# Late gate weights of a hybrid FoX/RWKV-7 layer: who issues the stores, when the first loads are issued, and which sums of weights a DMA makes

## The chip, the cores and the metric

The kernel runs on one core of one Trainium2 chip. The metric is the device time of one execution in microseconds; the figure that is compared is the median of several runs. For the kernel before it is 1662.03 us over 3 runs (1658.12 to 1666.03).

The engines go by the names of the profile: PE is TensorE's matmuls and PEld its weight loads, DVE is VectorE, ACT is ScalarE, POOL is GpSimd, and SP is SyncE, which here does nothing but issue DMAs. POOL and ACT can issue DMAs too. A DMA instruction stands in its engine's own in-order list: whatever it waits for, the instructions behind it on that engine wait for as well.

## The reference

One decoder layer in fp32 on 512 tokens of 2048 channels. Cut to what matters:

```python
h = rmsnorm(x, norm_gain)
u = h @ w_in                                    # 512x2048 by 2048x12488
u_fox, u_rwkv, g_a, g_b = split(u)
o_a = fox_attention(u_fox) * silu(z_a)          # 8 heads of 128, causal, forgetting
o_b = rwkv7_scan(token_shift(u_rwkv)) * silu(z_b)   # 16 heads of 64, with group norm
m = sigmoid(g_a) * (o_a @ w_proj_fox) + sigmoid(g_b) * (o_b @ w_proj_rwkv)
out = rmsnorm(x + m @ w_out, final_norm_gain)
```

The change concerns the 4096 columns of `w_in` that give g_a and g_b, the gates.

## The kernel before

Every fp32 matrix product is made of three products of fp32r tiles: each operand is split into a high part (rounded by ACT) and a low part (what is left, subtracted by DVE), and hi*hi, hi*lo and lo*hi are added up in PSUM. One product of a 128x256 block of h by a 256x512 block of weights so costs 12 matmuls of 128x128 by 128x512.

The order of the instructions of PE and SP is written by hand: generators yield after each matmul and a driver interleaves them. ACT, DVE and POOL are ordered by a scheduler that follows priorities; inside `tc.high_priority(offset=HP)` an instruction is ranked as if it stood 300 places earlier in the program. A DMA takes its place in the list of the engine that issues it by the same rule.

The program first makes the FoX and RWKV-7 branches, and then, towards 900 us, the gates, the two projections and the output product.

The gates come in four groups g of 1024 columns (g below 2 are gate B, the others gate A). A group is a 2x2 block product: two halves of the tokens, two halves of the contraction (1024 channels each) and two blocks of 512 columns. It is computed with seven products instead of eight (Strassen's scheme in Winograd's form). Two of the seven are made directly, in a stage of their own, while the last RWKV chains run: pieces of 128x512 of weights, loaded by SP, go through PE into c11, a quarter of the group. The first half of its contraction gives the partial sum p1, which is stored to DRAM (`p1_d`, L1075); after the second half tanh gives the finished quarter of the gate, stored to `sg_d` by `store_gate` (L926 to L928). Both are issued by Pool.

The other five products, the group of late units, are made by `gates_rest`. It starts once the last RWKV chain is done, since its buffers reuse that memory. A unit is 12 matmuls on a pair (hi, lo) of 128x1024 tiles, four units j=0..3 along the contraction for each of the products, which the code names by digits:

- unit 5: X = block 11 + block 12 of the weights, times the difference d1[j] of blocks of h (its tiles are named d_fqh, d_fql, d_fkh and so on, one pair for each j; d_fv stands for j=2 and d_fcb for j=3). Its PSUM tile is z.
- unit 7: block 12 + block 22, with PSUM tile x. After it block 22 is added to X.
- unit 6: that X (11 + 12 + 22), with PSUM tile y. After it Pool issues a DMA that accumulates block 21 onto X (L980).
- unit 3: block 22 once more, loaded a second time. Unit 4: X with 21 added.

In group 0 the order is (5, 7) for j=0..3, then 6 for j=0..3, then 3, then 4; the other groups go (5, 7, 6) per j. `load` (L946 to L961) brings a block of 256x512 as a tile of 128x2x512, 512 KB; the loads of the first four units (5 and 7 of j=0 and 1) are issued by Pool, the rest by SP. `prep` (L963 to L980) makes the sums and splits them (L423 casts to the high part h on ACT, L424 subtracts to the low part l on DVE). The driver prepares two units ahead and loads four ahead. The sums are `tt(V, ...)`, the helper at L482, on DVE:

```python
if p == "5":
    src = xs[j] = wp.tile([P, 2, 512], F32, tag="X", bufs=4, name=f"X_{g}{j}")
    tt(V, src, raw[n, "11"], raw[n, "12"], ALU.add)
...
if p == "7":
    tt(V, xs[j], xs[j], raw[n, "22"], ALU.add)
```

Behind units 6, 3 and 4, tanh of the sums with p1 (read back at L1002) gives the other quarters of the gate, each stored by `store_gate`. After the gates the projections `p` multiply by them: their weights are `whi_p`, `wlo_p`, and the gates are read back from `sg_d`. L136 is the matmul helper, L240 the load of a 128x512 piece (raw), L267 and L268 its split.

Of the kernel before, what the change touches and what calls it, by code (L numbers as in the profile page):

```python
# [9 lines left out]
F32 = mybir.dt.float32  # L10
F32R = mybir.dt.float32r
AF = mybir.ActivationFunctionType
ALU = mybir.AluOpType
# [4 lines left out]
P = 128  # L18
# [24 lines left out]
HP = 300  # L43
# [13 lines left out]
def hybrid_layer(  # L57
# [6 lines left out]
    nc = tc.nc  # L64
    V, S, G, PE = nc.vector, nc.scalar, nc.gpsimd, nc.tensor
# [62 lines left out]
    def mm(out, lhsT, rhs, start=True, stop=True, **kw):  # L128
        n = 1
        for d in rhs.shape[1:]:  # L130
            n *= d
        if rhs.dtype == F32R:
            clock[0] += max(n, 256) / 2370
        else:
            clock[0] += max(4 * n, {128: 514, 64: 230, 32: 150}.get(lhsT.shape[-1], 514)) / 2370
        PE.matmul(out, lhsT=lhsT, rhs=rhs, start=start, stop=stop, **kw)  # L136
# [5 lines left out]
    def ps_mm(name):  # L142
        return psm.tile([P, T], F32, tag="mm", bufs=2, name=name)
# [99 lines left out]
    def next_piece():  # L243


        i = used[0]
        used[0] += 1
        while len(raws) < min(i + (RAWS + 1 if i > 3 else 4), len(pieces)):
            raws.append(load_raw(*pieces[len(raws)]))
        split_pieces(i + (3 if i > 3 else 1))  # L250
        got = parts[i]
        parts[i] = None
        return got
# [61 lines left out]
    def gate_w(g, kb, cb, j, n=2):  # L315

        c0 = (GB0 if g < 2 else GA0) + g % 2 * 1024 + cb * 512
        r0 = (kb * KB + j * n) * P
        return w_in[r0:r0 + n * P, c0:c0 + 512]
# [24 lines left out]
    for hf in range(2):  # L344
        t = slice(256 * hf, 256 * hf + 256)
# [43 lines left out]
    for q in range(2):  # L389
        for col, base in ((0, -1), (64, 0)):  # L390
            m = smask[q * 64:(q + 1) * 64, col:col + 64]
# [29 lines left out]
    def split(hi, lo, a):  # L421

        S.copy(hi, a)  # L423
        V.tensor_tensor(lo, a, hi.bitcast(F32), ALU.subtract)  # L424
# [53 lines left out]
    sg_d = dram.tile([2, T, D], F32, name="sg_d")  # L478
    p1_d = dram.tile([4, 2, P, T], F32, name="p1_d")

    def tt(eng, o, a, b, op=ALU.mult):
        eng.tensor_tensor(o, a, b, op)  # L482
# [372 lines left out]
    def stage1():  # L855
# [69 lines left out]

        def store_gate(tile, g, th, cb, t):  # L926
            r0, c0 = 256 * th + P * t, g % 2 * 1024 + cb * 512
            G.dma_start(sg_d[g // 2][r0:r0 + P, c0:c0 + 512], tile)  # L928

        first_sums = [(w, j) for j in range(4) for w in ("d1", "s3")]  # L930
        late_stack = ExitStack()
# [11 lines left out]
        def gates_rest(wp):  # L943
# [5 lines left out]
            raw, xs, ready = {}, {}, {}  # L949
            at = [0]  # L950

            def load(upto):
                while at[0] < len(loads) and loads[at[0]][0] <= upto:
                    n, b = loads[at[0]]
                    at[0] += 1
                    g, p, j = units[n]
                    t = wp.tile([P, 2, 512], F32, tag=f"b{b}", bufs=3 if b == "22" else 2, name=f"b{b}_{g}{p}{j}")

                    (G if n < 4 else nc.sync).dma_start(
                        t, gate_w(g, int(b[0]) - 1, int(b[1]) - 1, j).rearrange("(k p) m -> p k m", p=P))  # L960
                    raw[n, b] = t  # L961

            def prep(n):  # L963
                g, p, j = units[n]
                if p == "5":
                    src = xs[j] = wp.tile([P, 2, 512], F32, tag="X", bufs=4, name=f"X_{g}{j}")
                    tt(V, src, raw[n, "11"], raw[n, "12"], ALU.add)
                elif p == "7":
                    src = raw[n - 1, "12"]
                    tt(V, src, src, raw[n, "22"], ALU.add)  # L970
                else:
                    src = raw[n, "22"] if p == "3" else xs[j]
                hi = wp.tile([P, 2, 512], F32R, tag="hi", bufs=3, name=f"h{g}{p}{j}")
                lo = wp.tile([P, 2, 512], F32R, tag="lo", bufs=3, name=f"l{g}{p}{j}")
                split(hi, lo, src)
                ready[n] = (hi, lo)
                if p == "7":
                    tt(V, xs[j], xs[j], raw[n, "22"], ALU.add)
                elif p == "6":
                    G.dma_start(xs[j], gate_w(g, 1, 0, j).rearrange("(k p) m -> p k m", p=P), accum_op=ALU.add)  # L980

            def ready_upto(n):
                while len(done) <= min(n, len(units) - 1):
# [4 lines left out]

            done = []
            load(1)  # L990
            ready_upto(1)
            yield
            left = [("s4", j) for j in range(4)]
            ev = lambda tag, nm: wp.tile([P, T], F32, tag=tag, bufs=4 if tag == "p1" else 2, name=nm)
            for n, (g, p, j) in enumerate(units):
                ready_upto(n + 2)
                load(n + 4)
                if (p, j) == ("5", 0):
                    pz = [ps_mm(f"z5_{g}_{t}") for t in range(2)]
                    p1 = [ev("p1", f"p1_{g}_{t}") for t in range(2)]  # L1000
# [12 lines left out]
                for t in range(2):  # L1013
                    for kk in range(2):
                        k = 2 * j + kk
# [38 lines left out]
        for g in range(4):  # L1054
            ps = [ps_mm(f"c11_{g}_{t}") for t in range(2)]
            for kb in range(2):
                for j in range(4):
                    ws = [next_piece(), next_piece()]
                    order = [(kk, t) for kk in range(2) for t in range(2)]
                    if j == 3:  # L1060
                        order = [(kk, t) for t in range(2) for kk in range(2)]
                    for kk, t in order:
                        k = 2 * j + kk
                        ah, al = (a[:, KB * kb + k, t * P:(t + 1) * P] for a in (hhi, hlo))
                        whi, wlo = (w[:, 0, :] for w in ws[kk])
                        for a, w, i in ((ah, whi, 0), (ah, wlo, 1), (al, whi, 2)):
                            mm(ps[t], a, w, start=kb == 0 and k == 0 and i == 0,
                               stop=kb == 1 and k == KB - 1 and i == 2, skip_group_check=True)
                            yield
                        if j == 3 and kk == 1:  # L1070
                            if kb == 0:
                                p1 = keep.tile([P, T], F32, tag=KEEP[t], name=f"p1_{g}_{t}")
                                with tc.high_priority(offset=HP):
                                    S.copy(p1, ps[t])
                                G.dma_start(p1_d[g, t], p1)  # L1075
                            else:
                                sg = keep.tile([P, T], F32, tag=KEEP[2 + t], name=f"c11_{g}_{t}")
                                with tc.high_priority(offset=HP):
                                    S.activation(sg, ps[t], AF.Tanh, scale=0.5)
                                store_gate(sg, g, 0, 0, t)  # L1080
                    if free["fox"] == 7 and first_sums:
                        sum_step(*first_sums.pop(0))
                    if g == 3 and kb == 1 and not first_sums:
                        sum_step("s2", j)
                    open_late()
# [58 lines left out]
        for br in range(2):  # L1144
            for n in range(4):
# [19 lines left out]
                for t in range(4):  # L1165
                    sg, m = sgs[br, n, t], ms_[n][:, t, :]
# [7 lines left out]

    result = []
    drive(stage1())
    mhi, mlo, turn_merged, four_banks = result

# [6 lines left out]
    for tb in range(4):  # L1185
        t = fin.tile([P, D], F32, tag="xo", bufs=4, name=f"xo_{tb}")
# [98 lines left out]
```

## Time and profile before

| | us |
|---|---|
| median of 3 runs | 1662.03 (1658.12 to 1666.03) |
| the profiled execution | 1661.46 |
| its span, first to last instruction | 1659.7 |

Shares of the span: PE 96% busy, PEld 79%, DVE 68%, ACT 47%, POOL 8%; the granted clock of TensorE is 0.99 on the mean.

The shares are means over stages with different limits, and the change touches the stretch from the last direct gate products (c, whose last matmul starts at 1054.69 us) to the end of group 0's late units and on to the projections. A row of the timeline gives the start, the length and the instruction, and in brackets the idle time of its engine before it with what ended it. PEclk is the granted clock of TensorE in shares of its full speed, the upper of its two levels (2.4 GHz; the lower is 1.2). "DMA to landing" is the time from the issue of a DMA to the arrival of its last byte. A DMA issued by Pool is in queue q0 of the page (software_dynamic), one issued by SP or ACT in a hardware queue.

### The profile page before, as it was taken

How to read it: one execution, taken by the hardware profiler on the slowest of the kernel's cores; microseconds unless marked ns; L12 is line 12 of the kernel's file. 1: busy time of each engine (PE TensorE's matmuls, PEld its weight loads, DVE VectorE, ACT ScalarE, POOL GpSimd, SP SyncE). 2: the span in 40 equal slices, each digit the busy share in tenths (PEclk: the TensorE clock that was granted, in tenths of full speed). 3: DMA queues.
4: the chain of work that ended last, by engine and by line, in shares of the span. 5: the costliest groups of instructions: out<-in, count | busy, mean ns of one | idle time of the engine just before them, and what ended most of it. 6: DMA issues, size and time to landing. Idle time of an engine off the chain costs nothing.

```text
span 1659.7 us, 23572 instructions
## 1 busy us (share of the span) xinstructions
PE 1600.1 (96%) x8378; PEld 1303.3 (79%) x8378; DVE 1127.0 (68%) x2173; ACT 771.8 (47%) x1503; POOL 132.9 (8%) x213
## 2 busy tenths in 40 slices
PE   6999899999999999999999899799999999999998
PEld 6888687787787887877878777588888787888886
DVE  6468678786787687777866859997887335544432
ACT  7533545636437446455364367554444223323322
POOL 3000000000100001000000000111111000001110
PEclk9999999999999999999999999899999999999999
DMA  5343334243333342342433366787776545463422
GB/s 168 98 104 86 82 83 106 70 112 87 93 92 85 92 113 75 95 100 68 113 84 90 102 186 186 248 251 200 235 235 172 184 153 155 151 216 122 139 83 102
DMA packets 234860, 216.39 MB, mean 130 GB/s; under 512 B 40326, under 2 KB 174062, under 8 KB 234102
## 3 DMA queue, kind: packets, MB, share of 16 engines
q1 hardware_dynamic: 222662, 179.73, 38.3%
q0 software_dynamic: 10640, 32.01, 7.0%
q10 hardware_dynamic: 1440, 3.15, 0.5%
q8 instruction: 66, 1.08, 0.3%
q14 instruction: 52, 0.43, 0.1%
HBM read 193.84 MB, written 20.99 MB: 129 GB/s over the span
## 4 chain that ended last, share of the span: by engine, by line
PE 60%; issue 15%; DVE 12%; DMA 5%; ACT 4%; POOL 2%; SPq 2%; POOLq 0%; ACTq 0%; DVEq 0%
PE o L136 11%; PE p L136 8%; PE u_fq L136 5%; PE u_fk L136 5%; PE c L136 5%; PE u_v L136 4%; PE u_z L136 4%; PE u_fv L136 3%; PE u_fz L136 3%; DVE Wt L482 3%; PE u_k L136 2%; DVE W L642 2%; PE u_r L136 1%; POOL X L980 1%; DMA lora<-in_rwkv_a_dram 1%
## 5 line engine op out<-in xcount | busy, mean ns | idle before, releaser
L136 PE MATMUL p<-whi_p,o 128*128 128x512 f32 x512 | 163.5, 396 | 0.1
L136 PEld LDWEIGHTS p<-whi_p,o 128*128 128x128 f32 x512 | 96.2, 188 | 22.2 <-ACT whi_p L267 1.0
L482 DVE TENSOR_TENSOR Wt<-W,Lt 128x16 f32<-128x16 f32 (+30 forms) x248 | 101.6, 410 | 6.2
L136 PE MATMUL p<-wlo_p,o 128*128 128x512 f32 x256 | 100.8, 394 | 1.1 <-DVE wlo_p L268 1.1
L268 DVE TENSOR_TENSOR wlo_p<-raw_p,whi_p 128x512 fp32r<-128x512 f32 x64 | 43.4, 691 | 85.6 <-ACT whi_p L267 85.5
L267 ACT ACTIVATE whi_p<-raw_p 128x512 fp32r<-128x512 f32 x64 | 40.4, 632 | 119.6 <-PE p L136 55.9
L268 DVE TENSOR_TENSOR wlo_o<-raw_o,whi_o 128x512 fp32r<-128x512 f32 x56 | 42.6, 762 | 78.0 <-ACT whi_o L267 77.5
L136 PE MATMUL o<-whi_o,mhi 128*128 128x512 f32 x224 | 87.6, 391 | 0.0
L136 PE MATMUL o<-whi_o,mlo 128*128 128x512 f32 x224 | 87.2, 389 | 0.0
L136 PE MATMUL o<-wlo_o,mhi 128*128 128x512 f32 x224 | 87.1, 389 | 0.0
L423 ACT CAST h<-X 128x1024 fp32r<-128x1024 f32 x48 | 50.5, 1052 | 65.0 <-PE z L136 22.3
L642 DVE TENSOR_REDUCE W<-Wt 128x8 f32<-128x16 f32 (+30 forms) x248 | 72.6, 293 | 5.6
L267 ACT ACTIVATE whi_o<-raw_o 128x512 fp32r<-128x512 f32 x56 | 35.3, 631 | 87.0 <-PE o L136 79.5
L424 DVE TENSOR_TENSOR l<-X,h 128x1024 fp32r<-128x1024 f32 x48 | 58.7, 1222 | 20.3 <-ACT h L423 20.1
L136 PE MATMUL c<-whi_g,hhi 128*128 128x512 f32 x128 | 53.4, 417 | 7.8 <-DVE fz L844 5.0
L719 ACT ACTIVATE pre<-SV,E 64x64 f32<-64x64 f32 x112 | 38.6, 345 | 41.8 <-DVE SV L732 40.9
L136 PEld LDWEIGHTS p<-wlo_p,o 128*128 128x128 f32 x256 | 48.1, 188 | 12.5 <-DVE wlo_p L268 2.1
L267 ACT ACTIVATE whi_g<-raw_g 128x512 fp32r<-128x512 f32 x64 | 40.2, 630 | 29.5 <-PE c L136 16.4
L423 ACT CAST h<-b 128x1024 fp32r<-128x1024 f32 x32 | 33.7, 1053 | 43.3 <-PE y L136 21.4
L268 DVE TENSOR_TENSOR wlo_g<-raw_g,whi_g 128x512 fp32r<-128x512 f32 x64 | 43.3, 685 | 14.0 <-ACT whi_g L267 13.8
L136 PE MATMUL c<-wlo_g,hhi 128*128 128x512 f32 x128 | 52.5, 410 | 0.0
L136 PE MATMUL u_fq<-hhi,whi_fq 128*128 128x512 f32 x128 | 52.4, 409 | 0.0
(428 smaller groups left out, 4711.8 us busy)
## 6 DMA issues: line engine op xcount, KB each, us to landing
b<-in_w_in_dram SPq DMA_DIRECT2D x58, 512.0 KB
raw_g<-in_w_in_dram SPq DMA_DIRECT2D x64, 256.0 KB
raw_o<-in_w_out_dram SPq DMA_DIRECT2D x56, 256.0 KB
raw_k<-in_w_in_dram SPq DMA_DIRECT2D x32, 256.0 KB
raw_r<-in_w_in_dram SPq DMA_DIRECT2D x32, 256.0 KB
raw_z<-in_w_in_dram SPq DMA_DIRECT2D x32, 256.0 KB
raw_v<-in_w_in_dram SPq DMA_DIRECT2D x32, 256.0 KB
raw_fq<-in_w_in_dram SPq DMA_DIRECT2D x32, 256.0 KB
```

The costliest lines, as they stand in the source:

```text
L136: PE.matmul(out, lhsT=lhsT, rhs=rhs, start=start, stop=stop, **kw)
L267: S.activation(whi, raw, AF.Copy)
L268: V.tensor_tensor(wlo, raw, whi.bitcast(F32), ALU.subtract)
L423: S.copy(hi, a)
L424: V.tensor_tensor(lo, a, hi.bitcast(F32), ALU.subtract)
L482: eng.tensor_tensor(o, a, b, op)
L642: V.tensor_reduce(W[:, :, i], tmp[:, :, 0:i + 1], AX.X, ALU.add)
L719: S.activation(pre[hs[q]], SV[hs[q], c, q, :], AF.Copy, scale=E1[hs[q], c, CH:CH + 1])
L980: G.dma_start(xs[j], gate_w(g, 1, 0, j).rearrange("(k p) m -> p k m", p=P), accum_op=ALU.add)
```

## The change

It has three parts.

- `store_gate` and the store of p1 are issued by ACT (`nc.scalar`) instead of Pool: 40 stores of 256 KB, 16 of them in the direct stage and 24 in the late groups.
- In group 0 block 11 is loaded straight into the tile X (four buffers, one for each j), and a second DMA, issued by Pool, accumulates block 12 onto it. Block 22 is accumulated onto X by a third one, also issued by Pool, once the split of unit 5 has read X. The DVE sums 11 + 12 and X + 22 of the four j, eight of 128x1024, are gone. Blocks 12 and 22 are still loaded plainly too, for unit 7. So there are eight accumulating DMAs more, and the number of plain loads stays.
- The loads of the first four units, with the accumulation that belongs to them, are issued at high priority.

TensorE's list is row for row the same in both kernels.

```diff
--- before.py
+++ after.py
@@ -925,7 +925,7 @@
 
         def store_gate(tile, g, th, cb, t):
             r0, c0 = 256 * th + P * t, g % 2 * 1024 + cb * 512
-            G.dma_start(sg_d[g // 2][r0:r0 + P, c0:c0 + 512], tile)
+            nc.scalar.dma_start(sg_d[g // 2][r0:r0 + P, c0:c0 + 512], tile)
 
         first_sums = [(w, j) for j in range(4) for w in ("d1", "s3")]
         late_stack = ExitStack()
@@ -954,15 +954,26 @@
                     n, b = loads[at[0]]
                     at[0] += 1
                     g, p, j = units[n]
-                    t = wp.tile([P, 2, 512], F32, tag=f"b{b}", bufs=3 if b == "22" else 2, name=f"b{b}_{g}{p}{j}")
-
-                    (G if n < 4 else nc.sync).dma_start(
-                        t, gate_w(g, int(b[0]) - 1, int(b[1]) - 1, j).rearrange("(k p) m -> p k m", p=P))
+                    onto = g == 0 and b == "11"
+                    if onto:
+                        t = xs[j] = wp.tile([P, 2, 512], F32, tag="X", bufs=4, name=f"X_{g}{j}")
+                    else:
+                        t = wp.tile([P, 2, 512], F32, tag=f"b{b}", bufs=3 if b == "22" else 2, name=f"b{b}_{g}{p}{j}")
+
+                    with tc.high_priority(offset=HP if n < 4 else 0):
+                        (G if n < 4 else nc.sync).dma_start(t, rows(g, b, j))
+                        if onto:
+                            G.dma_start(t, rows(g, "12", j), accum_op=ALU.add)
                     raw[n, b] = t
+
+            def rows(g, b, j):
+                return gate_w(g, int(b[0]) - 1, int(b[1]) - 1, j).rearrange("(k p) m -> p k m", p=P)
 
             def prep(n):
                 g, p, j = units[n]
-                if p == "5":
+                if p == "5" and g == 0:
+                    src = xs[j]
+                elif p == "5":
                     src = xs[j] = wp.tile([P, 2, 512], F32, tag="X", bufs=4, name=f"X_{g}{j}")
                     tt(V, src, raw[n, "11"], raw[n, "12"], ALU.add)
                 elif p == "7":
@@ -975,9 +986,12 @@
                 split(hi, lo, src)
                 ready[n] = (hi, lo)
                 if p == "7":
-                    tt(V, xs[j], xs[j], raw[n, "22"], ALU.add)
+                    if g == 0:
+                        G.dma_start(xs[j], rows(g, "22", j), accum_op=ALU.add)
+                    else:
+                        tt(V, xs[j], xs[j], raw[n, "22"], ALU.add)
                 elif p == "6":
-                    G.dma_start(xs[j], gate_w(g, 1, 0, j).rearrange("(k p) m -> p k m", p=P), accum_op=ALU.add)
+                    G.dma_start(xs[j], rows(g, "21", j), accum_op=ALU.add)
 
             def ready_upto(n):
                 while len(done) <= min(n, len(units) - 1):
@@ -1072,7 +1086,7 @@
                                 p1 = keep.tile([P, T], F32, tag=KEEP[t], name=f"p1_{g}_{t}")
                                 with tc.high_priority(offset=HP):
                                     S.copy(p1, ps[t])
-                                G.dma_start(p1_d[g, t], p1)
+                                    nc.scalar.dma_start(p1_d[g, t], p1)
                             else:
                                 sg = keep.tile([P, T], F32, tag=KEEP[2 + t], name=f"c11_{g}_{t}")
                                 with tc.high_priority(offset=HP):
```

Pool's list, from the store of the last RWKV output (ob_d) on, before. In the names, b11_050 is block 11 for group 0, unit 5, j=0; X_00 is the sum X of group 0, j=0; sg_d and p1_d are the gates and partial sums in DRAM.

```order
L771 DMA ob_d_559<-y_7_10521 128x512
L928 DMA sg_d_560<-c11_3_0_10726 128x512
L928 DMA sg_d_560<-c11_3_1_10735 128x512
L959 DMA b11_050_10543<-in_w_in_dram 128x2x512
L959 DMA b12_050_10545<-in_w_in_dram 128x2x512
L959 DMA b22_070_10547<-in_w_in_dram 128x2x512
L959 DMA b11_051_10745<-in_w_in_dram 128x2x512
L959 DMA b12_051_10747<-in_w_in_dram 128x2x512
L959 DMA b22_071_10755<-in_w_in_dram 128x2x512
L1002 DMA p1_0_0_10763<-p1_d_561 128x512
L1002 DMA p1_0_1_10764<-p1_d_561 128x512
L980 DMA X_00_10549<-in_w_in_dram 128x2x512
```

The same place of Pool's list in the changed kernel, where L964 is the plain load, L966 the accumulation of block 12, L990 that of block 22 and L1016 the read of p1:

```order
L771 DMA ob_d_559<-y_7_10521 128x512
L964 DMA X_00_10543<-in_w_in_dram 128x2x512
L964 DMA b22_070_10548<-in_w_in_dram 128x2x512
L964 DMA b12_050_10546<-in_w_in_dram 128x2x512
L966 DMA X_00_10543<-in_w_in_dram 128x2x512
L964 DMA X_01_10744<-in_w_in_dram 128x2x512
L964 DMA b12_051_10747<-in_w_in_dram 128x2x512
L964 DMA b22_071_10753<-in_w_in_dram 128x2x512
L966 DMA X_01_10744<-in_w_in_dram 128x2x512
L990 DMA X_00_10543<-in_w_in_dram 128x2x512
L1016 DMA p1_0_0_10762<-p1_d_561 128x512
L966 DMA X_02_10755<-in_w_in_dram 128x2x512
```

The two gate stores are gone from before the loads. The accumulations of block 12 stand between the loads, each behind the load whose tile it adds to. That of block 22 of j=0 (L990) stands ahead of that of block 12 of j=2 (L966); the next rows of the list, not shown, are the second read of p1, the accumulation of block 22 of j=1, and only then that of block 12 of j=3.

SP's list behind the last pieces of the direct stage, before:

```order
L240 DMA raw_p0_0_3_10714<-in_w_proj_rwkv_dram 128x512
L959 DMA b11_052_10757<-in_w_in_dram 128x2x512
L959 DMA b12_052_10759<-in_w_in_dram 128x2x512
L959 DMA b22_072_10785<-in_w_in_dram 128x2x512
L959 DMA b11_053_10807<-in_w_in_dram 128x2x512
L959 DMA b12_053_10809<-in_w_in_dram 128x2x512
L959 DMA b22_073_10829<-in_w_in_dram 128x2x512
L959 DMA b22_030_10922<-in_w_in_dram 128x2x512
```

And in the changed kernel:

```order
L240 DMA raw_p0_0_3_10713<-in_w_proj_rwkv_dram 128x512
L964 DMA X_02_10755<-in_w_in_dram 128x2x512
L964 DMA b12_052_10758<-in_w_in_dram 128x2x512
L964 DMA b22_072_10784<-in_w_in_dram 128x2x512
L964 DMA X_03_10804<-in_w_in_dram 128x2x512
L964 DMA b12_053_10807<-in_w_in_dram 128x2x512
L964 DMA b22_073_10827<-in_w_in_dram 128x2x512
L964 DMA b22_030_10918<-in_w_in_dram 128x2x512
```

SP's list has the same order: the load of block 11 of j=2 and 3 has become the load into X, and the first block of unit 3 (b22_030) stands behind the three loads of j=3 in both.

## Rows read from the trace of the kernel before

**Rows 1.** Stages: length, PE, PEld, DVE, ACT, POOL busy (count), PEclk, DMA share, GB/s.

```profile
1000.00:1050.00 50.00, 49.64 (x280) 39.46 (x279) 48.41 (x89) 36.86 (x69) 4.79 (x9) 1.00 0.67 198
1050.00:1100.00 50.00, 37.85 (x153) 30.22 (x152) 46.91 (x55) 22.82 (x29) 11.81 (x15) 0.86 0.76 228
1100.00:1300.00 200.00, 200.00 (x876) 164.04 (x875) 152.37 (x154) 94.02 (x109) 27.87 (x36) 1.00 0.76 225
```

**Rows 2.** Waits of PE, 930 to 1320 (us in total, times, longest).

```profile
PE z L136 <- ACT h L423: 11.2, 1, 11.2
PE p L136 <- DVE wlo_p L268: 0.6, 1, 0.6
```

**Rows 3.** Timeline of PE (start us, us, instruction, [idle before <- releaser]).

```profile
1066.28 0.79 PE L136 MATMUL z<-h,d_fqh 128*128 128x512 f32 x1 [11.20 <-ACT h L423]
1068.61 0.63 PE L136 MATMUL z<-h,d_fql 128*128 128x512 f32 x1
1072.45 0.63 PE L136 MATMUL z<-h,d_fql 128*128 128x512 f32 x1
1081.32 0.39 PE L136 MATMUL z<-h,d_fv 128*128 128x512 f32 x1
1086.81 0.39 PE L136 MATMUL z<-h,d_fcb 128*128 128x512 f32 x1
```

**Rows 4.** Timeline of POOL, issues of DMAs.

```profile
1053.78 0.54 POOL L771 DMA_DIRECT2D ob_d<-y  x1 [8.40 <-DVE y L770]
1056.54 4.31 POOL L959 DMA_DIRECT2D b<-in_w_in_dram  x6
1090.72 1.26 POOL L980 DMA_DIRECT2D X<-in_w_in_dram  x1 [28.78 <-DVE l L424]
1097.92 1.18 POOL L980 DMA_DIRECT2D X<-in_w_in_dram  x1 [1.41 <-DVE l L424]
```

**Rows 5.** Groups of DVE, 1060 to 1092 (busy us, mean ns); timeline of ACT.

```profile
L482 DVE TENSOR_TENSOR X<-b,b 128x1024 f32<-128x1024 f32 x4 | 4.9, 1221 | 2.1 <-DMA b<-in_w_in_dram 2.1
...
1065.18 1.05 ACT L423 CAST h<-X 128x1024 fp32r<-128x1024 f32 x1 [4.17 <-DVE X L482]
```

**Rows 6.** Landings: Pool's six loads (L959), accumulations to 1098 (L980), a store.

```profile
DMA to landing us min/median/max: 5.9/7.4/9.1
...
DMA to landing us min/median/max: 5.9/6.7/7.0
...
ob_d<-y POOLq DMA_DIRECT2D x8, 256.0 KB, 2.5
```

**Rows 7.** DMA by queue (packets, MB, share), 1065.6 to 1068 and 1092.5 to 1103.

```profile
DMA packets 258, 0.93 MB, mean 387 GB/s; under 512 B 31, under 2 KB 31, under 8 KB 258
q0 software_dynamic: 258, 0.93, 102.5%
...
DMA packets 980, 1.91 MB, mean 182 GB/s; under 512 B 49, under 2 KB 49, under 8 KB 980
q0 software_dynamic: 975, 1.90, 108.3%
```

**Rows 8.** The same columns for two windows of 5 us.

```profile
1075.00:1080.00 5.00, 5.00 (x24) 4.09 (x23) 5.00 (x5) 1.05 (x1) 0.00 (x0) 1.00 0.42 116
1085.00:1090.00 5.00, 5.00 (x23) 4.11 (x22) 5.00 (x6) 2.94 (x4) 0.00 (x0) 1.00 0.04 14
```

**Rows 9.** Timeline of SP, 1065 to 1068.

```profile
1065.19 0.38 SPq L959 DMA_DIRECT2D b<-in_w_in_dram  x1
```

**Rows 10.** PE after a shorter idle time, and the window around it.

```profile
941.60 0.80 PE L136 MATMUL c<-whi_g,hhi 128*128 128x512 f32 x1 [4.97 <-DVE fz L844]
...
940.00:950.00 10.00, 8.40 (x29) 6.85 (x30) 8.21 (x18) 1.99 (x4) 0.00 (x0) 0.66 0.30 79
```

**Rows 11.** Stores issued by ACT at the end (ns min/median/max).

```profile
L1253 ACTq DMA_DIRECT2D out_dram<-xo x8: 338/338/1667, 1639.4 to 1655.4; - x8
```

**Rows 12.** Timeline of DVE, 1285 to 1312.

```profile
1298.86 2.50 DVE L424 TENSOR_TENSOR o<-oraw,o 128x512 fp32r<-128x512 f32 x4 [7.86 <-DMA sg_d<-p]
```

## The prediction

> **What bounds the kernel now.** First the table of stages [rows 1]: TensorE is busy for all of the 200 us from 1100 to 1300 and for 49.6 of 50 us before 1050, but for only 37.9 of the 50 us from 1050 to 1100, at a granted clock of 0.86. Where TensorE is full, a microsecond can be won only by taking matmuls away, and the change leaves TensorE's list as it is. So what it does to the time is decided where TensorE waits, between the direct gate products and the group of seven. The waits [rows 2] name the place: one wait of 11.2 us of z (the product of unit 5) for ScalarE's h. The timeline [rows 3] shows it: z begins at 1066.28, and up to 1072.45 the matmuls follow each other at 0.427 us (1068.61 to 1072.45, nine of them) instead of the 0.228 us of the full stage (200 us by 876 matmuls) [rows 1]: the half clock after the idle time. From 1075 on TensorE never waits; unit (5, j=2) begins at 1081.32, unit (5, j=3) at 1086.81. The Pool timeline [rows 4] says why z is late: the six loads of late weights leave at 1056.54, behind the last RWKV store (1053.78) and two gate stores.
>
> **The change, part by part.**
>
> *Loads that leave earlier.* With the stores on ScalarE and the loads ranked up, the first load follows the RWKV store: 1053.78 + 0.54 = 1054.32, 2.2 us earlier. It can't go further up, since that store waits for DVE, whose last step there hangs on the same pieces of direct weights as before.
>
> *Two transfers in a row instead of two side by side.* Before, blocks 11 and 12 travelled together and DVE added them in 1.22 us; ScalarE's h began at 1065.18 [rows 5], 8.64 us after the first issue. Now 11 must land before Pool may issue the accumulating 12 on top of it. The first plain load landed after 5.9 us, an accumulating one on a quiet queue also after 5.9 (the least of six, and the least of four) [rows 6]. So X of j=0 is there at 1054.32 + 5.9 + 5.9 = 1066.1, and z, 1.1 us behind h's start as before, begins near 1067.3: 1.0 us later than now, although its first load left 2.2 earlier. Bounds: both as quick as the quickest Pool transfer of the page, a 256 KB store in 2.5 us [rows 6], plus 0.7 for the other 256 KB, give 3.2 each and z at 1061.8 (4.5 earlier); a second one of 7.0 (the slowest of the four) gives 1.1 more. I take 5.9, as it is the same kind of transfer of the same size.
>
> The Trainium skill (DMA: Bandwidth & Descriptors, section "Anatomy of one DMA — SWDGE (gpsimd) path") gives a Pool-issued transfer as about 2.0 us and its bytes at 436 GB/s. By that an estimate for 512 KB is 3.2 us and z would come 4.5 us earlier; the trace doesn't agree, with 5.9 for the first load of that size, and the measurement is used.
>
> *The DMA queue.* This is the main term. Per j the old kernel moved four blocks of 512 KB (11, 12, 22, and 21 accumulated); the new one moves 11, 12 and 22 just so, and again 12 and 22 on top of X: eight accumulating transfers more. Their price: the four of before leave from 1090.72 to 1097.92 and land 5.9 to 7.0 us later, so at 1096.6 to 1104.9, 2.77 us apart. The six plain loads leave from 1056.54 to 1060.1 (4.31 us for six issues) and land 5.9 to 9.1 later, 1062.4 to 1069.2, 1.36 us apart [rows 4, 6]. The queues say the same [rows 7]: 387 GB/s with the engines full of plain loads, 182 GB/s with them full (108%) of accumulating ones. So the eight cost 22 us of all DMA engines, in a stage where the idle share of the engines is small outside two windows (0.42 and 0.04 of 5 us [rows 8], some 7.7 us).
> Nor can other transfers slip past: SP issued a load at 1065.19 [rows 9], and between 1065.6 and 1068 the engines moved nothing but Pool's older ones [rows 7]. I treat the queue as first come, first served.
> Now count what must be through before unit (5, j=3) can start. The first accumulation can move data from about 1062 (11 landed at 1060.2, 1.2 us of issue, half a microsecond to start). Ahead of and with X of j=3 stand: six accumulations (12 for four j, 22 for j=0 and 1, which Pool issues before the last 12) x 2.77 = 16.6; nine loads (11, 12, 22 of j=1; 12 and 22 of j=2; three of j=3; the first of unit 3, which SP issues right behind them) x 1.36 = 12.2; two evicted partial sums of 256 KB, 1.4. Sum 30.2, so 1092.2; half a microsecond for the landing and 1.1 us for h give TensorE's start at 1093.8, against 1086.81 now: 7.0 late. Where Pool has to see a load land before it may issue, the queue can also run empty: between 0 and 3 x 3.1 us (5.9 less 2.77, for j=1 to 3). SP's loads stand in the queue at most of these moments, so I take 1. The term is +8.0, and it contains the 1.0 of the start, because a stall at j=3 swallows what came before. Its low end, accumulation at the price of a load: 15 x 1.36 and 1.4, is 21.8; X would be in time, and only the 1.0 is left. The high end is +16.
> Behind that point nothing gives it back: TensorE is full to 1300.
>
> *The clock.* Before j=3 TensorE would stand still for some 5 us (it ends the unit before near 1089). After 4.97 us of idleness at 941.60 the matmuls started at 0.80 us and the granted clock of that 10 us window was 0.66 [rows 10]; after the 11.2 us, a dozen matmuls cost 0.2 us more each [rows 3]. I put 12 x 0.2 = +2.4 on it; bounds 0 (no fall) and twice that (j=2 also).
>
> *Eight DVE sums less.* 8 x 1.22 = 9.8 us of DVE [rows 5]. Worth nothing: from 1075 TensorE didn't wait for DVE, though DVE was full.
>
> *Forty stores on ScalarE.* An issue there takes 0.34 us [rows 11]. Sixteen of them, 5.4 us, fall in the direct products, where ScalarE is busy for 36.9 of 50 us [rows 1]; weights are split three pieces ahead, and that hides them. Cost 0; 5.4 if each stood on the path. The other 24 fall where ScalarE is busy for 94 of 200 us. On SP the loads queued behind a store's semaphore are due several pieces later than the store; cost 0. At the end of the gates DVE now sits 7.86 us waiting for the last store to land, and TensorE 0.60 for DVE [rows 2, 12]; a store from ScalarE is out sooner: -0.6.
>
> **Sum.** +8.0 + 2.4 - 0.6 = +9.8 us on the profiled execution's 1661.46 (span 1659.7 and 1.8 around it), so 1671.3; the median of the runs shown is 1662.03, 0.6 above that execution, within the runs' own spread. Predicted: 1671.
>
> **Rivals.** *Only the start moves* (0.15): accumulation overlaps with plain loads, the queue keeps up and the early X's cover the rest. For it: before, 7.7 us of the engines were idle there; against: 22 us are added. +1.0 - 0.6: 1662.
> *An earlier start, faster* (0.07, and 0.03 for more): the loads leave 2.2 us earlier, and on a queue with three loads in it instead of six both transfers of X take 3.2 us; z begins 4.5 us earlier, and the half clock with it. For it: the store of 2.5 us; against: the first accumulation of before found an idle queue and took 5.9. 1661.5 - 4.5 - 0.6 = 1656.4. This is also what the skill's formula above would give, if it held for accumulation too. To pass 0.5% the stall itself (11.2 us) would have to go, which needs X before the RWKV store. It decides as soon as X of j=0 is ready before 1061.
> *Stalls at every j, and ScalarE's stores on the path* (0.10): Pool's list is in order, so an accumulation waiting for its load holds all that follow; with the queue empty three times (+9.3 instead of 1) or the stores' 5.4 in full: 1676 to 1680. Against: SP's loads fill the queue, and ScalarE has room.
> The forecast itself has 0.65, with +4 to +13, 1665 to 1675.
>
> **Chances.** What a measurement of this kernel can tell from no change is about 0.5%, 8.3 us: faster is below 1653.7, slower above 1670.3. Of the forecast's 0.65 about 0.48 lies above; with 0.10 of the stalls slower has 0.58. The first rival, the rest of the forecast and most of the early start lie within: 0.38. Faster 0.04. Range 1661 to 1678: below it lies the early start, above it the worst of the stalls.
>
> **What would show it.** Right: z begins near 1067; Pool shows accumulations waiting for landings; DMA share near 1 at about 200 GB/s from 1062 to 1093; TensorE idle some microseconds before d_fv and d_fcb, with a half clock after it; stage 1100 to 1300 still full, only later. Wrong: z before 1062, or no gap at d_fcb, or gaps in the direct products with ScalarE as their releaser.

## The result, and the profile after

The changed kernel takes 1677.24 us (median of 4 runs, 1674.46 to 1678.42), the kernel before 1661.63 us beside it: a ratio of 1.009, 95% interval 1.0063 to 1.0117, some 15 us slower (10 to 19). The forecast was 1671, with a range of 1661 to 1678: the time lies inside it, close to its upper end.

In the profiled execution (span 1675.9) TensorE's last matmul starts 16.15 us later than before. The starts of the same matmuls in both timelines share this out: 1.07 us were lost before the direct stage (nothing is changed there), 1.80 in the direct stage, 12.45 from its last matmul to the first of unit 6, 0.83 behind it. These are two executions; the start of the direct stage, ahead of which the program is the same in all fourteen kernels of this study, lies between 934.9 and 938.2 us in theirs, so a difference of a microsecond or two can be chance.

The table of stages, with the columns of [rows 1]:

```profile
1000.00:1050.00 50.00, 49.37 (x281) 39.43 (x281) 47.16 (x88) 34.28 (x67) 0.54 (x1) 1.00 0.66 191
1050.00:1100.00 50.00, 30.22 (x109) 22.71 (x107) 33.70 (x45) 18.65 (x26) 14.53 (x16) 0.80 0.97 267
1100.00:1300.00 200.00, 199.35 (x864) 163.44 (x865) 158.12 (x158) 94.65 (x109) 20.38 (x17) 0.99 0.79 222
```

The stage from 1050 to 1100 has lost: TensorE is busy for 30.2 us instead of 37.9, VectorE for 33.7 instead of 46.9, and the DMA engines have risen from 0.76 to 0.97. From 1100 on TensorE is full, as before.

The waits of TensorE from 930 to 1320 (us in total, times, longest), the answer to [rows 2], and the rows of its timeline with these waits, the answer to [rows 3]:

```profile
PE z L136 <- ACT h L423: 18.4, 3, 13.7
PE z L136 <- DVE l L424: 2.0, 3, 0.8
PE p L136 <- ACT whi_p L267: 1.3, 1, 1.3
PE dp L136 <- ACT GP L679: 1.2, 1, 1.2
```

```profile
1071.61 0.80 PE L136 MATMUL z<-h,d_fqh 128*128 128x512 f32 x1 [13.66 <-ACT h L423]
1089.97 0.50 PE L136 MATMUL z<-h,d_fv 128*128 128x512 f32 x1 [3.71 <-ACT h L423]
1091.23 0.54 PE L136 MATMUL z<-l,d_fv 128*128 128x512 f32 x1 [0.76 <-DVE l L424]
...
1099.39 0.50 PE L136 MATMUL z<-h,d_fcb 128*128 128x512 f32 x1 [1.03 <-ACT h L423]
1100.65 0.51 PE L136 MATMUL z<-l,d_fcb 128*128 128x512 f32 x1 [0.76 <-DVE l L424]
```

The one wait at z has become three: z (j=0) starts at 1071.61 instead of 1066.28, and TensorE now waits at d_fv (j=2) and d_fcb (j=3) too. Each time VectorE's low half of the same weights is late by another 0.5 to 0.8 us, and the matmuls run at the half clock for a while (the mean granted clock of the 50 us is 0.80, before 0.86).

Pool's and SP's timelines, the answers to [rows 4, 9]; L966 is the accumulation of block 12 onto X:

```profile
1056.54 0.54 POOL L771 DMA_DIRECT2D ob_d<-y  x1 [53.45 <-DVE y L770]
1057.07 0.74 POOL L964 DMA_DIRECT2D X<-in_w_in_dram  x1
...
1064.40 1.25 POOL L966 DMA_DIRECT2D X<-in_w_in_dram  x1 [5.19 <-DMA X<-in_w_in_dram]
1065.14 1.24 POOL L964 DMA_DIRECT2D X<-in_w_in_dram  x1
...
1072.50 1.21 POOL L966 DMA_DIRECT2D X<-in_w_in_dram  x1 [4.68 <-DMA X<-in_w_in_dram]
...
1074.53 2.23 POOL L966 DMA_DIRECT2D X<-in_w_in_dram  x1
...
1089.20 1.18 POOL L966 DMA_DIRECT2D X<-in_w_in_dram  x1 [7.13 <-DMA X<-in_w_in_dram]
```

```profile
1055.59 0.41 SPq L964 DMA_DIRECT2D X<-in_w_in_dram  x1
1074.04 0.99 SPq L964 DMA_DIRECT2D b<-in_w_in_dram  x2
1075.07 0.82 SPq L964 DMA_DIRECT2D X<-in_w_in_dram  x1
```

The first load leaves 0.53 us behind the RWKV store, as forecast. Its accumulation waits until 1064.40 for it to land, and the one of j=3 until 1089.20, since SP issued the load of that X only at 1075.07. The transfers by queue, 1076 to 1088 (the columns of [rows 7]), and the time from issue to landing of L966, the answers to [rows 6, 7]:

```profile
DMA packets 1598, 3.22 MB, mean 268 GB/s; under 512 B 93, under 2 KB 93, under 8 KB 1598
q0 software_dynamic: 781, 1.63, 67.7%
q1 hardware_dynamic: 817, 1.59, 40.8%
```

```profile
DMA to landing us min/median/max: 5.7/7.5/14.2
```

Pool's queue (q0, here accumulations and a read of p1 of 256 KB) and SP's (q1, plain loads) moved nearly the same bytes, 1.63 and 1.59 MB, in 781 and 817 packets, but Pool's took 68% of the engines' time and SP's 41%. Together they are more than full.

### The profile page after: what moved, and what is told of

It reads as the page before. It is cut to its first block, busy times and chain, and to the rows that moved or that the text cites. A ratio compares the mean times of both kernels' runs of the same rounds, so it can differ in the third digit from the quotient of the medians.

```text
span 1675.9 us, 23504 instructions
## 1 busy us (share of the span) xinstructions
PE 1603.5 (96%) x8378; PEld 1305.1 (78%) x8378; DVE 1118.9 (67%) x2165; ACT 770.4 (46%) x1503; POOL 120.4 (7%) x181
## 4 chain that ended last, share of the span: by engine, by line
PE 73%; DVE 11%; DMA 7%; ACT 4%; issue 3%; SPq 1%; POOL 0%; ACTq 0%; POOLq 0%; DVEq 0%
PE o L136 10%; PE p L136 8%; PE z L136 6%; PE u_fq L136 5%; PE u_fk L136 5%; PE y L136 5%; PE u_v L136 4%; PE u_z L136 4%; PE x L136 3%; PE u_fv L136 3%; PE u_fz L136 3%; PE c L136 3%; PE u_k L136 3%; DVE Wt L482 2%; PE u_r L136 2%
## 5 line engine op out<-in xcount | busy, mean ns | idle before, releaser
L268 DVE TENSOR_TENSOR wlo_p<-raw_p,whi_p 128x512 fp32r<-128x512 f32 x64 | 43.5, 691 | 89.7 <-ACT whi_p L267 89.7
L136 PEld LDWEIGHTS p<-wlo_p,o 128*128 128x128 f32 x256 | 48.1, 188 | 11.6 <-DVE wlo_p L268 1.1
L136 PE MATMUL u_fq<-hlo,whi_fq 128*128 128x512 f32 x128 | 52.4, 409 | 0.0
```

The lines of the kernel that those rows point to most:

```text
L268: V.tensor_tensor(wlo, raw, whi.bitcast(F32), ALU.subtract)
```

## The experiments

Each kernel was timed in five rounds beside the kernel before (1660.28 to 1660.61 us). The columns in the middle come from the profiled execution: z and unit 6 are the starts of their first matmuls, counted from the last direct matmul (c). There is one such execution of each kernel.

| kernel | median us | ratio, 95% | c to z | c to unit 6 |
|---|---|---|---|---|
| before | 1661.63 | | 11.6 | 37.6 |
| changed | 1677.24 | 1.009 (1.0063 to 1.0117) | 14.1 | 50.1 |
| e1, no accumulation | 1661.47 | 1.0012 (0.9998 to 1.0025) | 12.0 | 37.4 |
| e2, accumulation only | 1675.38 | 1.0088 (1.0074 to 1.0102) | 15.8 | 50.8 |
| e3, plain instead | 1673.28 | 1.0082 (1.0066 to 1.0098) | 12.8 | 44.7 |
| e4, half the bytes | 1674.03 | 1.0078 (1.006 to 1.0096) | 13.7 | 44.9 |
| e5, Pool's order | 1677.76 | 1.0106 (1.0084 to 1.0129) | 18.0 | 50.9 |
| e6, SP's order | 1678.08 | 1.0109 (1.0086 to 1.0132) | 15.4 | 48.5 |
| e7, both orders | 1676.25 | 1.0084 (1.0062 to 1.0106) | 20.2 | 48.8 |
| e8, early loads | 1668.00 | 1.0041 (1.0027 to 1.0054) | 12.1 | 38.5 |
| e9, block 12 only | 1672.27 | 1.0069 (1.0057 to 1.0082) | 14.2 | 44.9 |
| e10, block 22 only | 1662.84 | 1.0016 (1.0007 to 1.0025) | 11.8 | 38.5 |
| e11, early accumulation | 1676.81 | 1.0102 (1.0086 to 1.0118) | 11.7 | 43.5 |
| e12, VectorE's order | 1672.54 | 1.0072 (1.0059 to 1.0085) | 7.3 | 44.1 |

**Which part: e1 and e2.** e1 is the changed kernel with the sums back on VectorE:

```diff
-                    onto = g == 0 and b == "11"
+                    onto = False
...
-                if p == "5" and g == 0:
+                if False:
...
-                    if g == 0:
-                        G.dma_start(xs[j], rows(g, "22", j), accum_op=ALU.add)
-                    else:
-                        tt(V, xs[j], xs[j], raw[n, "22"], ALU.add)
+                    tt(V, xs[j], xs[j], raw[n, "22"], ALU.add)
```

> The changed kernel with both sums of weights back on VectorE (plain loads of blocks 11, 12, 22; no accumulating DMA but the old one of block 21). The stores stay on ScalarE. Queue theory (the eight accumulating transfers fill the DMA engines): nearly all of the loss goes; what stays is the direct stage, 1.6 us later by the trace, against loads that leave 2.2 us earlier behind the RWKV store: z near 1066, no wait of TensorE at d_fv or d_fcb, 1659 to 1663 us. Store theory (ScalarE's stores are the loss): 1670 or more, gaps in the direct products.

e2 keeps the sums and takes the rest back (stores to `G`, no priority):

> The kernel before with the accumulating sums of group 0 alone: stores stay on Pool, loads at their old rank. Queue theory: as late as the changed kernel or later, since the loads stand behind two gate stores again: 1676 to 1680 us, waits at z, d_fv and d_fcb. Store theory: 1666 or less.

Both times came out near what the queue theory says, though TensorE's waits in e2 fall at j=0 and j=1 (15.4 and 6.8 us) and not at d_fv and d_fcb, as was expected. The accumulations alone make about the whole loss; stores on ScalarE and the priority together can't be told from no change (by the interval they cost some 4 us at most). But e1 shows something else, in Pool's and VectorE's timelines (the row by itself is the sum X in the kernel before):

```profile
1054.96 0.54 POOL L771 DMA_DIRECT2D ob_d<-y  x1 [53.79 <-DVE y L770]
1055.49 4.26 POOL L964 DMA_DIRECT2D b<-in_w_in_dram  x6
```

```profile
1064.04 0.69 DVE L482 TENSOR_TENSOR st_s<-hhi 128x512 f32<-128x512 f32 x1
1065.18 1.23 DVE L482 TENSOR_TENSOR X<-b,b 128x1024 f32<-128x1024 f32 x1 [0.45 <-DMA b<-in_w_in_dram]
```

```profile
1063.86 1.23 DVE L482 TENSOR_TENSOR X<-b,b 128x1024 f32<-128x1024 f32 x1 [2.13 <-DMA b<-in_w_in_dram]
```

The first load leaves 0.53 us behind the RWKV store, 2.2 us sooner than before, and z isn't sooner at all. VectorE comes to the sum X straight from other work and waits for its blocks for 0.45 us only. It is done with that work 9.2 us after c; in the kernel before it was after 7.0, and then sat idle for 2.13 us. Why its list runs later in e1 was not tried.

**What about them: e3 and e4.** e3 drops `accum_op` from both new transfers (they overwrite X), e4 accumulates half of each tile; shown is block 12, the edit for block 22 is alike:

```diff
-                            G.dma_start(t, rows(g, "12", j), accum_op=ALU.add)
+                            G.dma_start(t, rows(g, "12", j))                                            # e3
+                            G.dma_start(t[:, 0, :], rows(g, "12", j)[:, 0, :], accum_op=ALU.add)        # e4
```

> The changed kernel, its eight new transfers with the same bytes, order, queue and waits, but overwriting X instead of accumulating onto it; X then holds one block and not the sum. Queue theory (an accumulating transfer costs twice a plain one): eight times 1.4 us of DMA time go, X of j=2 and 3 comes 8 to 11 us earlier, 1665 to 1669 us. Order theory (a transfer may be issued only when the one below it has landed, and Pool's list holds all behind it; the kind of transfer doesn't matter): 1674 to 1678 us.

> The changed kernel with each of the eight new accumulations on half the tile (128x512 instead of 128x2x512), so X lacks half of blocks 12 and 22; the number, order and waits of the instructions stay. Queue theory: eight times 1.4 us of DMA time go, as in the run without accumulation: 1665 to 1669 us. Order theory: 1673 to 1677 us.

Between the theories. From c to unit 6 each takes 5.2 to 5.4 of the 12.45 us away, less than the 8 to 11 of the queue theory; by their ratios they are only 0.0008 and 0.0012 under the changed kernel (1.3 to 2 us), with intervals that overlap (the profiled execution of e4, 1669.30, is among the fastest of its runs, 1669.13 to 1678.57). So the half of the loss that goes is read from two traces; the times do not show its size. At j=3, where the prediction's main term is worked out, z starts 35.5 us after c in e3, against 41.8 in the changed kernel and 32.1 in the kernel before. The queues of e3, 1076 to 1088:

```profile
q0 software_dynamic: 447, 1.56, 34.2%
q1 hardware_dynamic: 1584, 3.07, 69.5%
```

A plain transfer takes 34.2% of the engines for 1.56 MB, an accumulating one 67.7% for 1.63 MB: 1.9 times as much for a byte. So the price was right, but not all of the delay hangs on it. In e3, too, Pool stands still until a load has landed:

```profile
1064.28 0.71 POOL L966 DMA_DIRECT2D X<-in_w_in_dram  x1 [5.23 <-DMA X<-in_w_in_dram]
...
1085.45 0.71 POOL L966 DMA_DIRECT2D X<-in_w_in_dram  x1 [6.18 <-DMA X<-in_w_in_dram]
```

**The order of the lists: e5, e6, e7.** e5 issues Pool's six plain loads ahead of the accumulations, e6 lets SP load X of j=3 right behind that of j=2, e7 does both (shown is the edit of e5):

```diff
-                        if onto:
+                        if onto and n >= 4:                      # e5
                             G.dma_start(t, rows(g, "12", j), accum_op=ALU.add)
+                        if n == 3:
+                            for i in range(2):
+                                G.dma_start(xs[i], rows(g, "12", i), accum_op=ALU.add)
...
-            load(1)
+            load(3)
```

> The changed kernel, with the six plain loads of Pool (block 11 into X, 12 and 22 of j=0 and 1) issued first and the accumulations of block 12 of j=0 and 1 behind them; all transfers stay. In the changed kernel three of these loads stood behind an accumulation that waited 5.2 us. List theory (what costs the time is that a waiting DMA instruction holds those behind it in Pool's and SP's lists): j=1 and j=2 come 3 to 6 us earlier, the wait of X_03 in SP's list stays: 1668 to 1672 us. Queue theory (22 us more of DMA time): 1674 to 1678 us, as before this edit.

> The changed kernel, with SP's load of block 11 of j=3 into X moved from behind the loads of blocks 12 and 22 of j=2 (which wait for their buffers until 1074) to right behind that of j=2, which leaves at 1055.6; Pool's list stays as it is. List theory: X_03 lands before 1070, its accumulation no longer waits 7 us for it, the stall at d_fcb (1.0 us and the half clock behind) goes, that at d_fv stays: 1670 to 1674 us. Queue theory: 1674 to 1678 us.

> The changed kernel with both moves: Pool's six plain loads ahead of all accumulations, and X_02 and X_03 loaded by SP ahead of its waiting loads. Same transfers, same bytes, same stores. List theory: the waits of TensorE at j=1 to 3 go; what stays is the late start of z (2.5 us) and the direct stage (0.9 to 1.7): 1663 to 1667 us. Queue theory: the bytes are the same, so at most 3 us better than the changed kernel: 1674 to 1677 us.

The list theory fell: no reordering won more than its uncertainty. In e6 SP loads X of j=3 right behind that of j=2, and its accumulation leaves without waiting for a landing, 5.9 us sooner after c than in the changed kernel. Pool's timeline of e6, and below it TensorE's:

```profile
1082.33 1.67 POOL L967 DMA_DIRECT2D X<-in_w_in_dram  x1
...
1098.49 0.51 PE L136 MATMUL z<-h,d_fcb 128*128 128x512 f32 x1 [0.66 <-ACT h L423]
```

Still z of j=3 starts 41.9 us after c, as in the changed kernel (41.8): the accumulation now takes 15.0 us to land instead of 9.0. The waits of TensorE in e7 show the same:

```profile
PE z L136 <- ACT h L423: 19.8, 1, 19.8
PE z L136 <- DVE l L424: 3.0, 3, 1.9
```

The wait at ScalarE's h for j=2 and 3 is gone, but z alone now waits 19.8 us: the loads that went ahead lie in front of the first accumulation in the queue. The same transfers have to be through before unit 6 in any order, and c to unit 6 is 48.5 to 50.9 us in these three and the changed kernel.

**Which sum: e9 and e10.** Block 22 or block 12 goes back to VectorE (e9 makes only the last change of the diff of e1, e10 only the first two).

> The changed kernel with the sum of block 22 back on VectorE, so only block 12 is accumulated (four transfers of 512 KB more instead of eight). Queue theory (the loss grows with the DMA time that is added, about 0.55 us for each us): 11 us of it instead of 22, unit 6 starts 6 to 7.5 us later than before, counted from the end of the direct stage, 1667 to 1671 us. Serial theory (only the step 11, then 12, then the cast counts): 1674 to 1678 us, as the changed kernel.

> The changed kernel with the sum of blocks 11 and 12 back on VectorE, so only block 22 is accumulated, which TensorE needs no sooner than unit 6. Queue theory: again 11 us of DMA time more, which delay the plain loads of j=2 and 3: 1666 to 1671 us. Serial theory: nothing on the path to units 5 and 7 is added, 1660 to 1663 us, as without accumulation.

Neither theory has both: e9 lies near the queue theory (c to unit 6 7.3 us longer than before, the time 1 us above its bound), e10 inside the serial one. The waits of TensorE from 1060 to 1110, of e9 and of e10:

```profile
PE z L136 <- ACT h L423: 14.0, 2, 13.8
PE x L136 <- DVE l L424: 2.0, 2, 1.0
PE z L136 <- DVE l L424: 1.9, 3, 0.8
```

```profile
PE z L136 <- ACT h L423: 11.4, 1, 11.4
PE z L136 <- DVE l L424: 2.0, 2, 1.0
```

Four accumulations of block 22 add the same DMA time as four of block 12 and cost 0.9 us of c to unit 6 (0.0004 of the ratio, over e1): nothing before unit 6 reads their result, and X of units 5 still comes from plain loads. Those of block 12 cost 7.3 us. With both it is 12.45, more than the sum of the two: the accumulations of block 22 of j=0 and 1 then stand in Pool's list before that of block 12 of j=3, for which TensorE waits.

**Is z late for its loads: e8, e12, e11.** e8 is e1 with the last RWKV store taken off Pool's list:

```diff
-        G.dma_start(ob_d[p], t2)
+        (nc.scalar if p == 7 else G).dma_start(ob_d[p], t2)
```

> The run without accumulation (e1_no_accum), with the store of the last RWKV output issued by ScalarE too, so that nothing stands ahead of Pool's six loads but their own buffers (last read some 15 to 20 us before the direct stage ends). If the wait of 11.2 us at z is a wait for loads held in Pool's list, as the prediction has it, X of j=0 is on the chip before the direct stage ends, z starts by 1061 to 1064, as soon as VectorE's list comes to the sum, and the time is 1654 to 1659 us. Rival: VectorE's list is the bound there, or the loads take the DMA engines from the direct weights: 1660 to 1663 us.

Pool's and VectorE's timelines of e8, and the window from 1070 to 1080 (columns of [rows 1]):

```profile
1004.02 1.46 POOL L964 DMA_DIRECT2D b<-in_w_in_dram  x2
1035.12 2.81 POOL L964 DMA_DIRECT2D b<-in_w_in_dram  x4 [29.64 <-PE c L136]
```

```profile
1072.09 0.69 DVE L482 TENSOR_TENSOR st_s<-hhi 128x512 f32<-128x512 f32 x1
1072.70 1.22 DVE L482 TENSOR_TENSOR X<-b,b 128x1024 f32<-128x1024 f32 x1
```

```profile
1070.00:1080.00 10.00, 3.95 (x9) 2.77 (x10) 9.90 (x11) 3.76 (x4) 0.00 (x0) 0.50 0.18 52
```

The loads leave at 1004 and 1035, yet z still starts 12.1 us after c, at 1075.10. VectorE reaches the sum X at 1072.70 with no idle time right before it, and the DMA engines are busy for 18%. So z waits for VectorE's list. (The time is 1668 mostly since the direct stage took 124.8 us instead of 119.7 in e1. ScalarE waits there for pieces of direct weights for 5.0 us from 1030 to 1062, in e1 for 0.4; but in the changed kernel it is 5.8, with a stage of 120.7, so these waits alone don't explain the loss, and its cause stays open.) e12 takes VectorE's sums s2, which unit 6 needs, out of the way, and puts the first gate stores of groups 0 and 1 back on Pool. Of its edit against the changed kernel, the part of s2:

```diff
+                if n == 0:
+                    for i in range(4):
+                        sum_step("s2", i, lo if i == 0 else None)   # copies one column of lo first, so as to stand behind it
...
-                    if g == 3 and kb == 1 and not first_sums:
-                        sum_step("s2", j)
```

> No accumulation; the last RWKV store on ScalarE, the gate stores of groups 0 and 1 on Pool and the rest on ScalarE, and VectorE's sums s2 behind the split of unit 5, j=0. If VectorE's list is what z waits for once the loads are early: z 4 to 7 us after the direct stage (12.1 with the early loads alone), and 1656 to 1661 us, unless VectorE, full up to unit 6, gives the time back there: then 1660 to 1664 us with the wait at d_fv or at y instead. If it is not VectorE: z still 11 to 12 us after it, 1664 to 1668 us.

```profile
1065.71 0.79 PE L136 MATMUL z<-h,d_fqh 128*128 128x512 f32 x1 [6.92 <-ACT h L423]
```

```profile
1070.00:1080.00 10.00, 8.06 (x36) 6.22 (x35) 10.00 (x14) 2.19 (x3) 0.00 (x0) 0.99 0.50 161
1080.00:1090.00 10.00, 8.46 (x29) 5.79 (x28) 10.00 (x14) 3.34 (x4) 0.00 (x0) 0.84 0.43 154
```

z starts 7.3 us after c, near the 4 to 7 expected, but VectorE is full up to 1090 (10.00 of 10 us) and gives it all back and more: c to unit 6 is 44.1, and up to it TensorE waits 5.1 us more for VectorE's low halves l. The time was worse than either expectation. e11 is the changed kernel with the store of e8, Pool's order of e5 and VectorE's of e12:

> The changed kernel with three moves: the last RWKV store issued by ScalarE, so that Pool's loads and the accumulations of block 12 of j=0 and 1 leave during the direct stage; Pool's plain loads ahead of the accumulations; and VectorE's sums s2 (11 us, needed only by unit 6) behind the split of unit 5, j=0. If the wait at z is made by two things, the queue and VectorE's list, both are lifted: z 3 to 5 us after the direct stage instead of 12 to 14, no wait at d_fv or d_fcb, 1654 to 1660 us. Rival: the transfers take the DMA engines from the direct weights and the wait moves there: 1664 us or more.

The rival's time came true, not its mechanism. Pool's timeline of e11:

```profile
1003.03 0.74 POOL L966 DMA_DIRECT2D X<-in_w_in_dram  x1
...
1061.62 0.72 POOL L966 DMA_DIRECT2D b<-in_w_in_dram  x1 [24.55 <-DVE wlo_p L268]
...
1063.54 2.50 POOL L971 DMA_DIRECT2D X<-in_w_in_dram  x2 [0.30 <-issue]
```

X of j=0 was loaded at 1003, but the loads put ahead of its accumulation waited 24.55 us for a step of VectorE in the direct stage (wlo_p), and the accumulations could only leave at 1063.54. (The direct stage took 125.0 us here and 123.0 in e12, which move the RWKV store as e8 does.) No kernel of this study beats the one before; e1 can't be told from it.

## Why the prediction was right, and where it was not

The time lies in the range, and the main term came out near. Of the 16.15 us that the profiled execution lost, 9.8 were forecast. The other 6.35 are 1.07 ahead of the direct stage, where nothing is changed, 1.80 in the direct stage (forecast: 0), 2.05 from there to unit 6 (12.45 for 8.0 + 2.4) and 1.43 behind it (0.83 lost, 0.6 forecast as won). So the mechanism held, but the time stands above the 1665 to 1675 of the forecast itself, and that it is still inside the range is in part luck.

*The loads that leave earlier.* Right as to the 2.2 us. Wrong as to what they are worth: the prediction read the late z as a wait for loads. It is a wait for VectorE's list, with 2.1 us of loads on top; [rows 5] has it (2.1 us of idle time ended by a DMA, out of TensorE's 11.2), and e8 shows it, where the loads are long there.

*Two transfers in a row.* The mechanism is right, the size was small: z came 2.46 us later after c, not 1.0. The accumulation could leave 7.3 us after the plain load (1057.07 to 1064.40), not 5.9; two more of Pool's loads and SP's load of X of j=2 were under way with it, but that they made it slower was not tried. From the accumulation (1064.40) to ScalarE's h (1070.5) it is 6.1.

*The DMA queue.* The main term was +8.0 at j=3: z of j=3 starts 9.7 us later after c than before (41.8 for 32.1). The sum of what must be through held in the main. Accumulation costs 1.9 times a plain byte. And without the accumulations of block 22 (e9) z of j=3 starts 4.8 us sooner, where the prediction counted two of them ahead of it, 2 x 2.77 = 5.5.

The premise "I treat the queue as first come, first served" is wrong. From 1076 to 1088 the queues of Pool and SP moved 781 and 817 packets side by side. The Trainium skill (DMA: Bandwidth & Descriptors, section "Queues, rings and completion order") says that each DMA engine takes turns between the queues that have work, packet by packet; the trace agrees, with these two counts. [rows 7] seemed to say otherwise because its window ends at 1068. SP's load of 1065.19 moves its data after that, beside transfers that Pool had issued before it. The queues of the kernel before, 1068 to 1070:

```profile
q0 software_dynamic: 133, 0.41, 54.7%
q1 hardware_dynamic: 166, 0.34, 45.2%
```

That cost the forecast little, as its sum counts all that must be through before X of j=3, in whatever order (e5 to e7). Nor did the 1 us for waiting on landings (0 to 9.3) prove too small: the load of X of j=3 landed 14 us after its issue and its accumulation took another 9, but e6, without that wait, is as late.

What fails is the working of the term's low end: with accumulation at the price of a load, X would be in time and only 1.0 us lost. e3 has that price, and z of j=3 still starts 3.4 us later after c than before, unit 6 7.1. So by the traces 5.4 of the 12.45 us hang on the price of accumulating. What the rest hangs on, the bytes of eight more transfers or their issue behind a landing, stays open, and so does how the 7.3 us of block 12 divide: no run has its four transfers alone as plain ones.

*The clock.* One stall of 5 us was forecast at j=3, for 2.4 us; there were two, at j=2 and j=3, with short waits for ScalarE (3.71 and 1.03 us). Behind both, more than half of the dozen matmuls of z took 0.63 us instead of 0.39, so the low clock came twice: on the mean the granted clock is 0.74 from 1089 to 1095.5 and 0.76 from 1099 to 1106. Behind j=3 unit 6 fell back by another 2.7 us, 0.76 of it the wait for l: about the size forecast. What was lost behind j=2 adds nothing by itself, since TensorE then had to wait for X of j=3 all the same.

*Eight sums less.* Worth nothing for this kernel, as forecast, but the reason given (TensorE didn't wait for VectorE) holds only from 1075 on: ahead of it z waits for VectorE's list (e8). That the transfers take away what the change frees there is argued from e1 to e4, not tried by itself.

*The stores on ScalarE.* Nearly 0 in sum, as forecast (e1: 0.9998 to 1.0025). One sign of being wrong, a gap in the direct stage with ScalarE as its releaser, did appear: TensorE waits 1.2 us for ScalarE's GP (the dp row above) in all eleven kernels with all these stores on ScalarE, and in none of the other three (before and e2 with none, e12 with part of them there). From its first matmul to its last the stage takes 118.6 to 121.2 us with them and Pool's loads behind the RWKV store, 118.9 and 117.1 in the kernel before and e2: a loss of a microsecond or two is likely, but the spans overlap. At the projections the 0.60 us are gone in e1; VectorE's row, the answer to [rows 12], has 3.30 us of idle time instead of 7.86, ended by ScalarE and no longer by a store:

```profile
1294.91 2.50 DVE L424 TENSOR_TENSOR o<-oraw,o 128x512 fp32r<-128x512 f32 x4 [3.30 <-ACT o L423]
```

In the changed kernel a wait for whi_p (1.3 us) takes its place.

The rival "stalls at every j", with 1676 to 1680, came nearest in time; its mechanism did not decide. The order of Pool's list is worth nothing (e5 to e7), and the DMA engines, which it has standing empty three times, were busy for 0.97 of 1050 to 1100.

## What to carry to other kernels

A sum moved from an engine into an accumulating DMA cost about twice a plain transfer's DMA time here, on top of the load below it, which must land first. It was nearly free where nothing reads the result for long (block 22 alone, 0.9 us), and dear where a matmul waits for it and the DMA engines are full (block 12 alone, 7.3 us). Before a wait is put down to the transfer at the end of its chain, read how long the engine in between was idle for that transfer: 2.1 us of 11.2 here. Moving instructions about in the lists didn't help while the same bytes had to be through before the same unit (e5 to e7): when a queue is full, add up what must be through first, and ask about the order after that.

## What the runs showed of the hardware that was not expected

The row of an accumulating DMA of 512 KB on Pool is 1.2 us long, that of a plain one onto the same tile 0.71 us (1064.40 in the changed kernel, 1064.28 in e3). It does not hold Pool for so long: the load behind the first one starts 0.74 us after it, at 1065.14. The accumulations of block 12 in the changed kernel took 5.7 to 14.2 us from issue to landing; the longest of them stood beside other accumulations and SP's loads.
